# Two decoder layers: one pass over all tokens against two token halves, one behind the other

## The chip, the cores and the metric

The kernel runs on one core of one Trainium2 chip. The metric is the device time of one execution in microseconds (us); lower is better. All times below are of that core. Its engines are named as the profile names them: PE (TensorE, matmuls and transposes; PEld is its weight load), DVE (VectorE), ACT (ScalarE), POOL (GpSimd) and SP (SyncE). Each of them takes its instructions strictly in the order in which the program gives them; a DMA is put into a queue by one of the engines and then runs by itself.

## The reference

Two layers of a decoder run over 1024 prompt tokens and 8 sample tokens (one new token for each of 8 sequences with 1024 cached positions). Cut to what matters:

```python
for l in range(DEPTH):                       # 2 layers, D_MODEL 1024
    n = rmsnorm(yp, norm1[l])
    q, k, v, gq, gk, gv, glog, gg = project(n, w_in[l], ...)   # one input projection, 3088 columns
    od = diff_attn_prompt(q, k, v, lam)      # 4 heads, causal: softmax(q1 k1) - lam softmax(q2 k2), times v
    og, s_fin = gla_prompt(gq, gk, gv, glog) # 4 heads, gated linear attention, a state carried from token to token
    yp = yp + merge(od, og, gg, ...)         # per-head norms, silu gate, ONE output projection w_out
    yp = yp + ffn(yp, norm2[l], w_gu[l], w_down[l])   # SwiGLU, d_ff 2816
    # the 8 sample tokens go through the same weights; their attention reads
    # k and v of 1024 past positions out of a paged cache (page_table), their GLA a given state
```

What matters for the order of the work: the second half of the prompt (tokens 512 to 1023) needs keys, values and the GLA state of the first half. The first half needs nothing of the second. Everything but attention and GLA works on each token by itself.

## The kernel before

Every large product is made exact to nearly float32 by splitting both factors into a high part and the rest (`xH`, `xL` for activations; `wh`, `wl` for weights), and adding three products: high by high, rest by high, high by rest. ACT rounds a weight tile into `wh`, DVE subtracts to get `wl`. So a weight tile costs one DMA (`raw`), one or two ACT and DVE instructions, and then three matmuls for each block of 128 rows and each block of token columns. The "dense" work below means these split products: input projection, output projection and feed-forward network (FFN). "Mix" means attention, GLA and what belongs to the 8 sample tokens (decode): reading cache pages, scores, softmax, weighted values.

A layer (`layer`) runs for all 1032 tokens in four phases.

- `phase_d`: head by head, the q, k, v columns of the input projection (`psq`, 128 tokens by 384 columns, 9 token tiles), QK norm and rotary (`qk`), transposes (`tpqk`), and causal attention of each 128-token tile (`attend`: scores `psS`, softmax in `sc`, transposes `tpw`, values `po`). Attention of a tile is written LAG = 2 tiles behind its projection. Page work of the decode (`decode_k`: `kpg` pages loaded by SP, multiplied by POOL, summed by DVE) is spread between by KRATE.
- `phase_g`: GLA. Products `psqk`, `psv`, `psgg` (the dense part of it), and `gla_a`, `gla_o`, `decode_softmax`, `decode_v`, `sample_gla`, called in an order written out by hand. Matmuls `psA`, `poG`, `puG`, `psov`, `psgn` are its mix.
- `out_phase`: output projection into `psf` (three blocks of 344 token columns, CH = 344), residual added.
- `ffn_phase`: chunks of 3 or 4 blocks of 128 hidden features: gate, up, Silu, down, all into `psf`. Weight tiles come through `prep_tile` (L977): rings of 3 `raw`, 3 `wh` and 2 `wl` tiles.

In `phase_d` and `phase_g` the engines have dense and mix work side by side. In `out_phase` and `ffn_phase` there is dense work alone. The order on each engine follows the order of the code, with a scheduler that lets an instruction that is free go ahead of one that waits; once fixed, it doesn't change at run time. Nearly all DMAs, weights, cache pages and results, go through SP's queue; POOL issues two.

Of the kernel before, what the change touches and what calls it, by code (L numbers as in the profile page):

```python
# [28 lines left out]
CH = TOK // 3  # L29
# [8 lines left out]
NPB = 5  # L38
KPB = 4
LAG = 2  # L40
GRH = 3
KRATE = (0, 2, 1, 3)
# [8 lines left out]
BIG = 3.0e38  # L51

# [6 lines left out]
def hybrid_kernel(  # L59
# [9 lines left out]
    w_queues = (ACT, SP, SP)  # L69

    const = ctx.enter_context(tc.tile_pool(name="const", bufs=1))
    dram = ctx.enter_context(tc.tile_pool(name="dram", bufs=1, space=DRAM))

    def cst(name, shape, dt=F32):
        return const.tile(shape, dt, name=name, tag=name)

# [9 lines left out]
    last_silu = []  # L86
    preload = []

    def load_ln_exp():
        with ExitStack() as st:  # L90
            if last_silu:
                st.enter_context(tc.issue_after(last_silu[-1].ins))
            preload.append(ACT.preload_act_table_set("natural_log_exp_and_others"))

    def after_preload(ins):
        tc.add_manual_dep(ins.ins, preload[-1].ins.name,
                          mybir.DependencyInfo(mybir.DependencyClass.NoSync, mybir.DependencyReason.DATA), reason="act table")

# [6 lines left out]
    def bc(ap, shape):  # L105
        return ap.to_broadcast(shape)

# [12 lines left out]
    xH = cst("xH", [P, KD, TOK], F32R)  # L120
    xL = cst("xL", [P, KD, TOK], F32R)
    xs = cst("xs", [P, KD, 40], F32R)
    POOL.memset(f(xs), 0.0)
    ssq = cst("ssq", [P, TOK])
    rstd = cst("rstd", [P, TOK])
    rcol = cst("rcol", [P, NT + 1])
    r2 = cst("r2", [P, NT + 1])
    lnr = cst("lnr", [P, NT + 1])
    lnm = cst("lnm", [P, NT + 1])

# [3 lines left out]
    load_ln_exp()  # L134
# [14 lines left out]
    ssqc = cst("ssqc", [P, NT + 1])  # L149

    def col_stats(rows, cols, src, scale):
        after_preload(act(lnm[rows, cols], src, AF.Ln, scale=scale, bias=eps_t[rows]))
        act(rcol[rows, cols], lnm[rows, cols], AF.Exp, scale=-0.5)
        act(r2[rows, cols], lnm[rows, cols], AF.Exp, scale=-1.0, bias=nln64[rows])
        act(lnr[rows, cols], lnm[rows, cols], AF.Copy, scale=-0.5)

    def rms_rows(pool, psp, tag, ttag="nrt"):
        for t in range(3):
            sl = slice(t * CH, (t + 1) * CH)
            ps = psp.tile([P, 512], F32, name="nrm", tag=tag)  # L160
            mm(ps[:, :CH], ones_dm, ssq[:, sl], True, True)
            tmp = pool.tile([P, CH], F32, name="nrt", tag=ttag, bufs=1)
            after_preload(act(tmp, ps[:, :CH], AF.Ln, bias=eps_t))
            act(rstd[:, sl], tmp, AF.Exp, scale=-0.5)

    def rms_cols(pool, psp, tag):
        ps = psp.tile([P, 512], F32, name="nrc", tag=tag)
        for i in range(NT):
            mm(ps[:, i:i + 1], ssq[:, i * P:(i + 1) * P], ones_dm[:, 0:1], True, True)
        mm(ps[0:NB, NT:NT + 1], ssq[:, SEQ:TOK], ones_dm[:, 0:1], True, True)  # L170
        for rows, cols in ((slice(0, P), slice(0, NT)), (slice(0, NB), slice(NT, NT + 1))):
            col_stats(rows, cols, ps[rows, cols], 1.0)

    def prep_cols(wps, l, c0, ns, w, step, q=SP, gr=False, width=None):
        Hs, Ls = [], []
        n = ns * w + (RANK if gr else 0)
        width = width or n
        for k in range(KD):
            raw = wps[0].tile([P, width], F32, name="raw", tag="raw", bufs=4)
            if ns == 1:  # L180
                q.dma_start(raw, w_in[l, k * P:(k + 1) * P, c0:c0 + w])
            else:
                b0 = c0 - c0 % step
                q.dma_start(raw[:, :ns * w].rearrange("p (s c) -> p s c", s=ns),
                            w_in[l, k * P:(k + 1) * P, b0:b0 + ns * step]
                            .rearrange("p (s c) -> p s c", s=ns)[:, :, c0 % step:c0 % step + w])
            if gr:
                q.dma_start(raw[:, ns * w:n], w_in[l, k * P:(k + 1) * P, C_GR:C_GR + RANK])
            wh = wps[1].tile([P, width], F32R, name="wh", tag="wh", bufs=9)
            wl = wps[2].tile([P, width], F32R, name="wl", tag="wl", bufs=9)  # L190
            g = g1c[:, l, k:k + 1]
            act(wh[:, :n], raw[:, :n], AF.Copy, scale=g)
            stt(wl[:, :n], raw[:, :n], g, f(wh[:, :n]), ALU.mult, ALU.subtract)
            Hs.append(wh)
            Ls.append(wl)
        return Hs, Ls

    def gemm_tok(ps, n, Hs, Ls, i):
        for k in range(KD):
            if i < NT:  # L200
                ts = slice(i * P, (i + 1) * P)
                mm(ps[:, :n], xH[:, k, ts], Hs[k][:, :n], k == 0, False)
                mm(ps[:, :n], xL[:, k, ts], Hs[k][:, :n], False, False)
                mm(ps[:, :n], xH[:, k, ts], Ls[k][:, :n], False, k == KD - 1)
            else:
                mm(ps[0:40, :n], xs[:, k, :], Hs[k][:, :n], k == 0, False)
                mm(ps[0:40, :n], xs[:, k, :], Ls[k][:, :n], False, k == KD - 1)

    def gemm_feat(ps, c0, Hs, Ls, t):
        ts = slice(t * CH, (t + 1) * CH)  # L210
        for k in range(KD):
            mm(ps[:, :CH], Hs[k][:, c0:c0 + P], xH[:, k, ts], k == 0, False)
            mm(ps[:, :CH], Hs[k][:, c0:c0 + P], xL[:, k, ts], False, False)
            mm(ps[:, :CH], Ls[k][:, c0:c0 + P], xH[:, k, ts], False, k == KD - 1)

    scr_q = [dram.tile([NB, H * 2 * DK], F32, name=f"scr_q{l}") for l in range(DEPTH)]
    scr_sn = [dram.tile([NB, 2 * H], F32, name=f"scr_sn{l}") for l in range(DEPTH)]
    scr_gv = [dram.tile([NB, H * DV], F32, name=f"scr_gv{l}") for l in range(DEPTH)]
    scr_v = [dram.tile([NB, H * DV], F32, name=f"scr_v{l}") for l in range(DEPTH)]
    scr_x = [dram.tile([KD, P, TOK], F32, name=f"scr_x{l}") for l in range(DEPTH)]  # L220
    scr_oh = [dram.tile([H, P, SEQ], F32, name=f"scr_oh{l}") for l in range(DEPTH)]
    scr_ol = [dram.tile([H, P, SEQ], F32, name=f"scr_ol{l}") for l in range(DEPTH)]

    smp = ctx.enter_context(tc.tile_pool(name="smp", bufs=1))

    page_dma = []

    def layer(l):
        sn = smp.tile([NB, 2 * H], F32, name="sn", tag="sn")
        osd = smp.tile([P, H, NB], F32, name="osd", tag="osd")  # L230
        if l:
            sample_cols()

        with ExitStack() as octx:
            with ExitStack() as mix:
                pgp = mix.enter_context(tc.tile_pool(name="pgp", bufs=1, reuse_waits="tile", side="right"))
# [96 lines left out]
    def phase_d(l, dctx, sn, pgp):  # L333
# [241 lines left out]
        for u in todo:  # L575
            decode_k(*u)
# [649 lines left out]
```

## Time and profile before

| what | value |
|---|---|
| median of 3 runs | 2929.18 us (2926.89 to 2933.85) |
| the profiled execution | 2924.06 us; its span, first to last instruction, 2922.3 us |
| mean granted TensorE clock | 0.975 of full speed |
| busy share of the span | PE 94%, PEld 90%, DVE 55%, ACT 39%, POOL 14% |
| DMA | 236.34 MB, 81 GB/s on the mean |

Read the table as an average over unlike stages: each layer has some 603 us of `phase_d` and `phase_g`, where all engines are busy, and some 850 us of `out_phase` and `ffn_phase`, where PE alone is. "Busy" counts a matmul that runs at half clock for as long as it takes, so a busy PE is not PE at its best.

### The profile page before, as it was taken

The page shows a single profiled execution, that of the slowest core. Times are in us where ns is not written, and L with a number is a line of the kernel's source. Part 1 is how long each engine was busy: PE and PEld are TensorE (multiplying, and loading weights), DVE is VectorE, ACT ScalarE, POOL GpSimd, SP SyncE. Part 2 cuts the span into 40 slices and gives each one's busy share as a digit, 9 for nine tenths or more (in the row PEclk, how much of TensorE's full clock was granted, in tenths as well). Part 3 has the DMA queues.
Part 4 walks back from the last instruction along what each step waited for, and adds up shares of the span by engine and source line. Part 5 has one row for each costly group of instructions (what it writes and reads, how often), then busy time and mean ns, then how long its engine had stood idle before and what let it go on. Part 6 is the DMA issues. An engine that isn't in the chain of part 4 may idle for free. (4 is left out here: it accounts for less than half of the span.)

```text
span 2922.3 us, 46249 instructions
## 1 busy us (share of the span) xinstructions
PE 2753.5 (94%) x16910; PEld 2616.2 (90%) x16910; DVE 1615.0 (55%) x3159; ACT 1146.4 (39%) x2960; POOL 404.9 (14%) x340
## 2 busy tenths in 40 slices
PE   8998898889999999999988988988899999999999
PEld 7787788789999999999977777877899999999998
DVE  7898887964333333333478988689543333333332
ACT  7787535652111111112377874356421111111112
POOL 1232423311000000000113233143110000000000
PEclk9999999999999999999999999999999999999999
DMA  4343414453011121212023333235531121211112
GB/s 136 91 132 92 136 37 117 129 177 134 27 55 57 33 62 33 62 30 69 23 85 96 109 112 106 55 112 149 165 123 37 40 62 33 62 37 55 47 40 77
DMA packets 320134, 236.34 MB, mean 81 GB/s; under 512 B 26122, under 2 KB 293642, under 8 KB 319906
## 3 DMA queue, kind: packets, MB, share of 16 engines
q1 hardware_dynamic: 311138, 229.16, 26.5%
q10 hardware_dynamic: 8704, 4.20, 0.6%
q8 instruction: 133, 2.18, 0.3%
q14 instruction: 95, 0.78, 0.1%
q0 software_dynamic: 64, 0.03, 0.0%
HBM read 201.33 MB, written 31.98 MB: 80 GB/s over the span
## 5 line engine op out<-in xcount | busy, mean ns | idle before, releaser
L78 PE MATMUL psf<-xH,wh 128*128 128x344 f32 x2112 | 676.1, 320 | 0.0
L78 PE MATMUL psf<-xH,wl 128*128 128x344 f32 x2112 | 674.7, 320 | 0.0
L78 PE MATMUL psf<-xL,wh 128*128 128x344 f32 x2112 | 674.5, 320 | 0.0
L84 ACT ACTIVATE wh<-raw 128x512 fp32r<-128x512 f32 (+1 forms) x304 | 178.1, 616 | 1113.1 <-PE psf L78 1099.6
L78 PEld LDWEIGHTS psf<-xH,wh 128*128 128x128 f32 x2112 | 396.6, 188 | 0.6 <-ACT xH L84 0.4
L78 PEld LDWEIGHTS psf<-xH,wl 128*128 128x128 f32 x2112 | 396.9, 188 | 0.2
L78 PEld LDWEIGHTS psf<-xL,wh 128*128 128x128 f32 x2112 | 396.6, 188 | 0.4
L78 PE MATMUL psf<-hh,wl 128*128 128x344 f32 x1056 | 338.5, 321 | 0.0
L78 PE MATMUL psf<-hh,wh 128*128 128x344 f32 x1056 | 338.3, 320 | 0.0
L78 PE MATMUL psf<-hl,wh 128*128 128x344 f32 x1056 | 338.2, 320 | 0.0
L100 DVE TENSOR_TENSOR acc<-psf,acc 128x1032 f32<-128x1032 f32 x96 | 118.3, 1233 | 301.6 <-PE psf L78 301.6
L100 DVE TENSOR_TENSOR tb<-psf,rstd 128x1032 f32<-128x1032 f32 x44 | 54.2, 1233 | 389.2 <-PE psf L78 389.2
L100 POOL TENSOR_TENSOR kpg<-kpg,qbd 128x512 f32<-128x512 f32 x128 | 170.6, 1340 | 438.2 <-DMA qbd<-scr_q 147.9
L100 DVE TENSOR_TENSOR wl<-raw,wh 128x512 fp32r<-128x512 f32 (+1 forms) x304 | 204.9, 690 | 13.1 <-PE psf L78 12.1
L100 DVE TENSOR_TENSOR sa<-psf,rstd 128x1032 f32<-128x1032 f32 x44 | 54.2, 1233 | 274.8 <-PE psf L78 274.8
L78 PEld LDWEIGHTS psf<-hh,wh 128*128 128x128 f32 x1056 | 198.6, 188 | 0.2 <-DVE acc L100 0.2
L78 PEld LDWEIGHTS psf<-hh,wl 128*128 128x128 f32 x1056 | 198.4, 188 | 0.3 <-DVE wl L100 0.3
L78 PEld LDWEIGHTS psf<-hl,wh 128*128 128x128 f32 x1056 | 198.3, 188 | 0.0
L78 PE MATMUL psq<-wh,xH 128*128 128x384 f32 (+1 forms) x512 | 183.1, 358 | 5.3 <-ACT v L84 3.9
L78 PE MATMUL psq<-wl,xH 128*128 128x384 f32 (+1 forms) x512 | 183.2, 358 | 2.7 <-DVE wl L103 2.7
L78 PE MATMUL psq<-wh,xL 128*128 128x384 f32 (+1 forms) x512 | 181.7, 355 | 0.0
L78 PE MATMUL psf<-oL,wh 128*128 128x344 f32 x384 | 126.2, 329 | 0.0
(319 smaller groups left out, 5468.4 us busy)
## 6 DMA issues: line engine op xcount, KB each, us to landing
raw<-in_w_gu SPq DMA_DIRECT2D x88, 512.0 KB
kpg<-in_cache_k SPq DMA_DIRECT2D x256, 128.0 KB
page<-in_cache_v SPq DMA_DIRECT2D x128, 256.0 KB
raw<-in_w_down SPq DMA_DIRECT2D x64, 256.0 KB
raw<-in_w_in SPq DMA_DIRECT2D x64, 192.0 KB
scr_x<-og SPq DMA_DIRECT2D x16, 516.0 KB
acc<-scr_x SPq DMA_DIRECT2D x16, 516.0 KB
raw<-in_w_in SPq DMA_DIRECT2D x64, 128.0 KB
```

The lines of the kernel that those rows point to most:

```text
L78: PE.matmul(out, lhsT=lhsT, rhs=rhs, start=start, stop=stop, skip_group_check=True)
L84: return ACT.activation(out, in_, func, **kw)
L100: (eng or DVE).tensor_tensor(out, a, b, op=op)
```

## The change

The tokens are split into two halves, X = 0 (512 tokens) and X = 1 (512 and the 8 sample tokens, 520 columns, taken as two blocks of 260). Each phase is a function of layer and half: `phase_p` (all of the input projection: q, k, v and the GLA columns), `phase_t` (the mix: `attention` and `gla`, decode with X = 1), and `phase_of` (output projection and FFN). The mix of one half is issued beside dense work of the other. Since the halves of two phases now live side by side, nothing is handed over in SBUF any more. `phase_p` writes q, k, v, GLA inputs and gates to DRAM (`scr_qk`, `scr_v`, `scr_g`, `scr_gv`, `scr_gr`, `scr_gg`); `phase_t` reads them back through POOL's queue (`TQ = POOL`) and writes its results split into `scr_oh`, `scr_ol`; `phase_of` reads those on SP's queue (16 loads). The residual stays in DRAM (`scr_x`).

Where an instruction of the mix falls between dense ones is decided by a number, its priority: `dense(us)` and `mix(us)` advance two clocks by the length that the author writes for each piece, and `mix_window(start, rate)` sets where the mix of a half begins on the dense clock and how fast it runs against it.

The weights are loaded and split once for each half, so twice a layer. PSUM is split into two double banks for dense work (`psD`) and four banks for mix (`psM`). Rings are shorter: LAG 2 to 1, `kpg` 4 to 3, `page` 5 to 4, `raw` of `prep_tile` 3 to 2. FFN chunks are 4, 4, 4, 4, 4, 2 blocks, and the Silu of each chunk is followed by a reload of the table of Ln and Exp on ACT (49 table loads in place of 4).

```diff
-NPB = 5
-KPB = 4
-LAG = 2
+NPB = 4
+KPB = 3
+LAG = 1
-KRATE = (0, 2, 1, 3)
...
+HALF = 512
+COLS = (HALF, HALF + NB)
+WM = HALF + NB
+SUBS = (((0, HALF),), ((0, WM // 2), (WM // 2, WM)))
+TILES = ((0, 1, 2, 3), (4, 5, 6, 7, NT))
+TICK = 20
+WINDOWS = ((20.0, 1.0), 0.7, 1.0, 0.7)
...
+    def dense(us):
+        tc.cur_priority = 1000 + int(clock["dense"] * TICK)
+        clock["dense"] += us
+
+    def mix(us):
+        tc.cur_priority = 1000 + int(clock["mix"] * TICK)
+        clock["mix"] += us * clock["rate"]
+
+    def mix_window(start, rate):
+        clock["mix"], clock["rate"] = start, rate
...
+    TQ = POOL
...
+                def start():
+                    for x in range(X + 1):
+                        kt[x] = ap.tile([P, 2, 512], F32R, name="kt", tag="kt", bufs=X + 2)
+                        vt[x] = ap.tile([P, 4, DV], F32, name="vt", tag="vt", bufs=X + 2)
+                        TQ.dma_start(vt[x], scr_v[l][x][h].rearrange("(i p) d -> p i d", p=P))
+                    if X:
+                        TQ.dma_start(f(kt[0]), scr_kt[l][h])
...
+    def phase_t(l, X, start, rate):
+        mix_window(start, rate)
...
+            attention(l, X, sall)
+            gla(l, X, sall)
...
-        raw = wps[0].tile([P, KD, P], F32, name="raw", tag="raw", bufs=nb)
-        SP.dma_start(raw[:, :nk, :], src)
+        raw = wps[0].tile([P, KD, P], F32, name="raw", tag="raw", bufs=2)
+        SP.dma_start(raw[:, :nk, :], src.rearrange("(k p) c -> p k c", p=P))
...
+                for k in (3, 0, 1, 2, 4, 5, 6, 7):
+                    SP.dma_start(f(oH[:, k, :W]), scr_oh[l][X][k])
+                    SP.dma_start(f(oL[:, k, :W]), scr_ol[l][X][k])
...
+                    si = act(sa[:, :n, :W], sa[:, :n, :W], AF.Silu)
+                    load_ln_exp(si)
...
+        phase_p(0, 0, s, xH, xL)
+        phase_t(0, 0, *WINDOWS[0])
+        phase_p(0, 1, s2, xH2, xL2)
+    t = clock["dense"]
+    phase_t(0, 1, t, WINDOWS[1])
+    s = phase_of(0, 0)
+    phase_p(1, 0, s, xH, xL)
+    t = clock["dense"]
+    phase_t(1, 0, t, WINDOWS[2])
+    s = phase_of(0, 1)
+    phase_p(1, 1, s, xH, xL)
+    t = clock["dense"]
+    phase_t(1, 1, t, WINDOWS[3])
+    phase_of(1, 0)
+    phase_of(1, 1)
```

So T(0,0) is issued beside P(0,1), T(0,1) beside OF(0,0) and P(1,0), T(1,0) beside OF(0,1) and P(1,1), T(1,1) beside OF(1,0), and OF(1,1) by itself (P, T and OF for the three phases, with layer and half).

On PE, before, this is the place where layer 0 goes from GLA to its output projection: the gate products `psgg`, the last decode values (`psov`) and norms (`psgn`, `pson`), and `psf` is the output projection.

```order
2291 L78 MATMUL psgg<-xL,wh 128x344
2292 L78 MATMUL psov<-ones_66,vacc 128x1 x8
2293 L78 MATMUL psgn<-gsq,ones_dv 128x16
2294 L78 MATMUL psf<-oH_9006,wh 128x344
2295 L78 MATMUL psgn<-gsq,ones_dv 128x512
2296 L78 MATMUL psf<-oL_9008,wh 128x344
2297 L78 MATMUL psf<-oH_9006,wl 128x344
2298 L78 MATMUL psf<-oH_9006,wh 128x344
```

After the change, PE at the start of OF(0,0): `psd` is any dense product, here the output projection of half 0, and `tpqk`, `psS` are transposes and scores of attention of half 1.

```order
2020 L96 MATMUL psd<-xH_170,wl 128x260
2021 L96 MATMUL psd<-oH,wh 128x512
2022 L96 MATMUL psd<-oL,wh 128x512
2023 L96 MATMUL psd<-oH,wl 128x512
2024 L96 MATMUL psd<-oH,wh 128x512
2025 L99 MATMUL tpqk<-ident,qk 128x128 x2
2026 L96 MATMUL psd<-oL,wh 128x512
2027 L96 MATMUL psd<-oH,wl 128x512
2028 L96 MATMUL psd<-oH,wh 128x512
2029 L99 MATMUL tpqk<-ident,qk 128x128 x2
2030 L96 MATMUL psd<-oH,wh 128x512
2031 L96 MATMUL psS<-kt,qhh 128x512
```

Mix steps that stood beside input projections now stand one by one between dense products of the output projection and the FFN, and dense products behind such a step come after it on PE.

On POOL, before, this is the end of the decode values of layer 0 and the start of its FFN (`ssq` are sums of squares for the next norm, `wa` a gate weight).

```order
79 L100 TENSOR_TENSOR vacc<-vacc,vaccp 128x512
80 L100 TENSOR_TENSOR vaccp<-vaccp,page 128x512 x3
81 L100 TENSOR_TENSOR vacc<-vacc,vaccp 128x512
82 L100 TENSOR_TENSOR ssq<-ssq,og 128x1032 x7
83 L100 TENSOR_TENSOR ssq<-ssq,acc 128x1032 x4
84 L532 DMA wa_15744<-in_w_a 16x256
```

After, POOL in T(0,1): `qk`, `vt`, `kt` are the handover read back from DRAM, `qbd` the query of a sample token, `kpg` the multiplication of cache pages.

```order
95 L537 DMA vt<-scr_v_126 128x4x128
96 L544 DMA qk<-scr_qk_123 128x256 x2
97 L539 DMA kt<-scr_kt_120 128x1024
98 L105 TENSOR_TENSOR kpg<-kpg,qbd 128x512 x4
99 L509 DMA qbd<-scr_q_112 128x256
100 L105 TENSOR_TENSOR kpg<-kpg,qbd 128x512
101 L544 DMA qk<-scr_qk_123 128x256
102 L105 TENSOR_TENSOR ssq<-ssq,nsq 128x512
103 L105 TENSOR_TENSOR kpg<-kpg,qbd 128x512 x3
```

DMA issues that POOL did not have before stand behind its multiplications; POOL has 486 rows in place of 162, about 290 of them DMA issues.

On SP, after, within the FFN of OF(0,0): `raw` is a weight tile of the down product, `page` a value page of the cache. Before, no page load stands between two weight loads of the FFN.

```order
2153 L493 TENSOR_LOAD pt_sb
2154 L493 ISA x2
2155 L494 ISA
2156 L494 DMA page<-in_cache_v 128x512
2157 L1007 DMA raw<-in_w_down 128x4x128
2158 L493 TENSOR_LOAD pt_sb
2159 L493 ISA x2
2160 L494 ISA
2161 L494 DMA page<-in_cache_v 128x512
```

Weight loads now wait in SP's queue behind page loads; at 19 places 4 to 9 of them, and at one place, before the first weight of OF(0,1), 50, stand between two weight loads.

## Rows read from the trace of the kernel before

**Rows 1.** The page's first part: the span, and each engine's busy time and share.

```profile
span 2922.3 us, 46249 instructions
...
PE 2753.5 (94%) x16910; PEld 2616.2 (90%) x16910; DVE 1615.0 (55%) x3159; ACT 1146.4 (39%) x2960; POOL 404.9 (14%) x340
```

**Rows 2.** Windows by stage: length, busy us (instructions) of each engine, clock, DMA share, GB/s.

```profile
0.00:603.00 603.00, 529.67 (x3105) 465.27 (x3105) 506.57 (x1256) 398.94 (x1242) 174.25 (x160) 0.95 0.39 111
...
1461.00:2064.00 603.00, 523.28 (x3050) 459.36 (x3051) 505.18 (x1235) 391.48 (x1214) 179.75 (x158) 0.94 0.38 110
...
2166.00:2916.00 750.00, 749.02 (x4764) 746.23 (x4764) 244.03 (x275) 134.34 (x194) 0.00 (x0) 1.00 0.18 54
```

**Rows 3.** PE's timeline: start, duration, line, operation, tile, shape.

```profile
202.90 0.34 PE L78 MATMUL psq<-wl,xH 128*128 128x384 f32 x1
...
205.70 0.34 PE L78 MATMUL psq<-wh,xH 128*128 128x384 f32 x1
...
220.82 0.39 PE L78 MATMUL psS<-kt,qhh 128*128 128x512 f32 x1
221.05 0.40 PE L78 MATMUL psS<-kt,qlz 128*128 128x512 f32 x1
...
369.49 0.28 PE L78 MATMUL psv<-wh,xL 128*128 128x256 f32 x1
...
370.78 0.28 PE L78 MATMUL psv<-wh,xH 128*128 128x256 f32 x1
...
372.35 1.13 PE L78 MATMUL psA<-xqz,gD 128*128 128x128 f32 x8
373.24 0.36 PE L78 MATMUL psv<-wl,xH 128*128 128x256 f32 x1
```

**Rows 4.** The chain that ended last, in order of time: start, us, what.

```profile
2064.62 90.01 PE psf L78 x570
...
2166.67 706.18 PE psf L78 x4483
...
2911.47 3.79 PE psf L78 x24
```

**Rows 5.** PE's waits in 1461:2064: who waited for whom; total us, times, longest.

```profile
PE tpqk L81 <- DVE qk L100: 14.6, 12, 4.6
PE tpw L81 <- DVE sc L103: 9.1, 14, 2.5
```

**Rows 6.** Windows of two short stretches, columns as in group 2.

```profile
146.00:219.00 73.00, 68.93 (x379) 59.32 (x378) 69.55 (x201) 62.05 (x216) 27.37 (x20) 1.00 0.47 131
600.00:610.00 10.00, 4.02 (x25) 3.97 (x23) 8.63 (x17) 5.75 (x17) 4.62 (x4) 0.66 1.00 341
```

**Rows 7.** Groups by line and shape: count, busy us, mean ns, idle before.

```profile
L100 DVE TENSOR_TENSOR wl<-raw,wh 128x512 fp32r<-128x512 f32 x272 | 187.4, 707 | 13.1 <-PE psf L78 12.1 <-issue 0.8
L84 ACT ACTIVATE wh<-raw 128x512 fp32r<-128x512 f32 x272 | 161.3, 626 | 953.1 <-PE psf L78 939.7 <-issue 7.6 <-DMA raw<-in_w_gu 3.5
L100 DVE TENSOR_TENSOR acc<-psf,acc 128x1032 f32<-128x1032 f32 x96 | 118.3, 1233 | 301.6 <-PE psf L78 301.6
L93 ACT ACT_TABLE_LOAD x2 | 2.6, 1283 | 0.8 <-PEq L1210 0.7
```

**Rows 8.** One line's operations: duration in ns, least, median, longest; first, last start.

```profile
L262 SPq DMA_DIRECT2D page<-in_cache_v x128: 332/333/742, 422.9 to 2044.7; - x128
...
L261 SPq TENSOR_LOAD <-pt_sb x384: 261/268/872, 35.3 to 2043.9; - x192
L261 SPq FUSED_REGOPS  x384: 147/152/181, 35.9 to 2044.2; - x192
```

**Rows 9.** POOL's own DMAs and its page multiplication, columns as in group 8.

```profile
L532 POOL DMA_DIRECT2D wa<-in_w_a x2: 546/609/672, 3.3 to 1451.2; - x2
...
DMA to landing us min/median/max: 2.0/3.0/4.0
...
L100 POOL TENSOR_TENSOR kpg<-kpg,qbd x128: 1261/1288/2254, 110.6 to 1788.2; 128x512 f32<-128x512 f32 x128
```

More of the change, by code (lines that the diff above doesn't have):

```diff
@@ L106, in bc, with load_ln_exp, after_table @@
         return ap.to_broadcast(shape)
+    clock = {"dense": 0.0, "mix": 0.0, "rate": 1.0}
+    def dense(us):
[6 more added lines that the diff above has]
+        clock["mix"], clock["rate"] = start, rate
+    def load_ln_exp(after=None):
+        with ExitStack() as st:
+            if after is not None:
+                st.enter_context(tc.issue_after(after.ins))
+            return ACT.preload_act_table_set("natural_log_exp_and_others")
+    first_table = load_ln_exp()
+    def after_table(ins):
+        tc.add_manual_dep(ins.ins, first_table.ins.name,
+                          mybir.DependencyInfo(mybir.DependencyClass.NoSync, mybir.DependencyReason.DATA), reason="act table")
     ident = cst("ident", [P, P])
@@ L148, in hybrid_kernel @@
     subg1 = cst("subg1", [P, DEPTH])
[L149 to L226, printed above, removed]
@@ new lines, in attention, with pop @@
+            pending = []
+            def pop():
+                us, fn = pending.pop(0)
+                mix(us)
+                fn()
+                decode_some(4)
+            for h in (3, 0, 1, 2):
+                start, prep, attend, finish = head(h)
+                mix(1)
+                start()
+                for i in range(4):
+                    mix(2.5)
+                    prep(i)
+                    pending.append((2 + 1.6 * (TILES[X][i] + 1), lambda a=attend, i=i: a(i)))
+                    while len(pending) > LAG:
+                        pop()
+                pending.append((4, finish))
@@ new lines, in hybrid_kernel @@
+    s = Stats()
+    with ExitStack() as bs:
+        xb = left(bs, "xb")
+        xH2 = xb.tile([P, KD, WM], F32R, name="xH2", tag="xH2")
+        xL2 = xb.tile([P, KD, WM], F32R, name="xL2", tag="xL2")
+        dense(1)
+        load_x(0, xb, s, xH, xL)
+        rms_load(s, 0)
+        with ExitStack() as ls:
+            load_consts(ls)
+        s2 = Stats()
+        clock["dense"] = 70
+        dense(0)
+        load_x(1, xb, s2, xH2, xL2)
+        rms_load(s2, 1)
+        sample_cols(xH2, xL2)
+        clock["dense"] = 10
+        phase_p(0, 0, s, xH, xL)
+        phase_t(0, 0, *WINDOWS[0])
+        phase_p(0, 1, s2, xH2, xL2)
```

1598 lines of the change are left out of this document (812 added, 786 removed).

## The prediction

> **What bounds the kernel now.** I read the page's first part first: PE is busy 94% of the span, DVE 55%, ACT 39% [rows 1]. At face value little is left to win. But busy is not work: a matmul at half clock counts double. So next come the windows by stage [rows 2]. From 2166 on PE is busy 749.02 of 750 us at clock 1.00 with 4764 matmuls, that is .157 us each, and nothing else is half as busy: here PE's own speed is the bound and nothing can be gained without taking matmuls away. In attention and GLA (0 to 603, and 1461 to 2064 for layer 1) PE is busy 523 to 530 of 603 us, and at clock .94 to .95. The chain of waits says the same: in the last stage two pieces of PE alone carry nearly all of it [rows 4]. So all that can be won lies in the two stretches of 603 us.
>
> How much? PE's timeline gives the step of each kind of matmul when they follow each other without a gap [rows 3]: sixteen steps of 384 columns from 202.90 to 205.70 are .175 us each, 512 columns (220.82 to 221.05) .23, eleven steps of 256 columns .117, eight of the small GLA ones .111. A layer has 832 matmuls of 384 columns (146 us), 416 of 256 columns (49), 576 of 344 columns (90), and mix (attention, GLA, decode, transposes) that comes to about 170 by counting at .1 to .23 each, an estimate. That is 455 us of work in a stretch of 603: **148 us lost in each layer, 296 in both**. The rest of the run, 2924 - 2 x 603 = 1718, is 1673 of `psf` work (10,656 matmuls at .157), some 20 of transposes and norms, 8 at the start of the first output projection (600:610 has PE at 4.02 of 10), some 3 at the norms, and 9 at the end (last matmul over at 2915.26, span 2922.3, run 2924.06) [rows 1, 4, 6]. So work is about 2 x 455 + 1693 = 2,600, and the account closes to within 10 us.
>
> Why is it lost there? PE's waits there are short and many, and nearly all on DVE or ACT: `tpqk` on `qk`, `tpw` on the softmax [rows 5]. PE, in order, waits in the middle of attention's chain of small steps, and with a granted clock of .94 on the mean, between its levels of 1.2 and 2.4 GHz, it runs a part of the stretch at the lower one [rows 2]. Where enough dense work stands between, it needn't be so: from 146 to 219, attention beside projections, PE is busy 68.93 of 73 us at clock 1.00, though DVE is busy 69.55 [rows 6]. So 5.6% lost is possible beside attention, against 148 of 603, 25%, as things are.
>
> **The change part by part.**
>
> *Matmuls.* The same products over the same columns. A weight tile's three products over a third of the tokens cost 3 x .157 = .47 us for 344 + 344 + 344 columns; in halves they are one of .23 (512) and two of 260, which by the 256-column step are .12 each: .47. No change. Work stays at 2,600.
>
> *Weights twice.* Each weight tile is split a second time. FFN and output projection: 272 pieces of DVE at 707 ns and of ACT at 626 ns [rows 7]; with the smaller forms I add 303 us to DVE and 261 to ACT. Forty-five more table loads at 1283 ns are 58 on ACT [rows 7]. DVE comes to about 1,920 us, ACT to 1,465, of some 2,840: both below PE. DVE is hidden behind PE as long as no stretch has it near full. Adding the order's rows at these durations, the opening stretch has DVE 297 beside PE 320, T(0,1) 440 beside 515, T(1,1) 600 beside 800: no stretch where DVE is the longer. DMA grows from 236 to about 400 MB (102 of weights, 60 of handover), 140 GB/s on the mean, where a window shows 341 [rows 6].
>
> *Where the loss goes.* Mix beside dense now spans PE work of 320 + 515 + 493 + 800 = 2,128 us, with OF(1,1), 473, alone after it. The gap per mix step can be filled by dense products of the FFN, which need nothing of it. Best case by rows 6: 5.6 of 94.4, so 126 us over the contested stretch. Worst that is no mechanism of its own: the 296 stay. I take **148**, half of today's, close to the fed slice but not at it, because LAG is 1 in place of 2 and rings are shorter.
>
> *Starts of OF.* Four in place of two, each with 16 loads of 256 KB, 4.2 MB; at 341 GB/s [rows 6] that is 12.3 us. In layer 0 before, the same start cost 8. Now a mix may run meanwhile, in three of four. Bounds 0 and 12.3; I take 10 each, **40**.
>
> *Norm joints.* Four pairs in place of two, each half as long; before, the gate products of the first chunk cover them. **10** for all.
>
> *Page loads ahead of weights.* On SP one page costs .333 + .268 + .152 = .75 us [rows 8], so eight between two weight loads, as the order shows, are 6.0 us. The PE work of a gate unit is 24 x .23 = 5.5, of a down unit 12 x .23 = 2.8, and two `raw` tiles stand ahead. Gate units hide it; down units lose some .5 to 1 at each of 19 places: **16**. A page load that has to wait for a free buffer makes it more; that is in the slower rival.
>
> *Start and end.* Before, the first wait for tokens is in the 296; **13** more for P(0,0), whose weights are first split with no mix beside them, and **9** at the end as before.
>
> *Handover.* Results are stored well before they are read (on PE, T(0,1) ends at row 3933, the first product of OF(0,1) that uses it stands at 4851), so the way through DRAM itself costs nothing. What POOL pays: its two DMA issues took .61 us of the engine, landing 3.0 later [rows 9]; 290 are 177 us more on POOL, beside 405 busy [rows 1]. That is hidden behind a span of 2,840 unless a read is late: 3.0 us for each of 4 tiles of a head is covered by rings of 3.
>
> Rows 9 also hold the one hint against it: `kpg` takes 1,288 ns on the median, 2,254 at most, 1 us more, about one long DVE instruction (the split of 512 columns is .707, the eviction of 1,032 is 1.233) [rows 7]. The Trainium skill, page SBUF — State Buffer, sections "SBUF: two separate sides" and "Who interferes with whom", says that POOL itself makes the descriptors of the DMAs that it issues, and that it is locked out while some forms of DVE's instructions run. The spread of `kpg` agrees with such a lock; no run here shows it for a DMA. By the rule these 290 would be the wrong queue.
>
> **Sum.** 2,600 + 148 + 40 + 10 + 16 + 13 + 9 = 2,836; I say **2,840**. The profiled run before took 2924, so 3% less; the median shown is 2929.18, 5 us above that run, within what runs differ. What a measurement can tell from no change is about 0.2%, 6 us.
>
> **The rivals.**
>
> *A. Better overlap.* The fed slice repeated, and OF starts hidden by mix: loss of 74 (a quarter), starts 0: 2,836 - 74 - 40 = 2,722. For it: FFN products are 2,000 us of cover for 340 of mix. Against it: the slice is 73 us picked as the best one, and 126 is what it gives when scaled. I put 2,700 to 2,790 here. Chance .12.
>
> *B. Slower: PE's queue waits inside the mix.* The order is fixed by lengths that the author wrote in; PE has one queue. A mix step whose softmax is 3 us late now stops dense work behind it, FFN too, which before ran at 749 of 750. DVE also has FFN evictions of up to 1.23 us [rows 7] and twice the splits in its queue between the steps of a softmax, so each step of attention's chain comes later than before. If the 296 stay, the sum is 2,836 + 148 = 2,984; it decides against the change once the loss is over 148 + 88 = 236, 80% of today's (the sum then is 2924). Page loads that wait in front of weights add to it. For it: DVE at 85% beside T(0,1). Against it: the fed slice had DVE at 95% and lost 5.6%. Chance .23.
>
> *C. Slower: POOL's queue.* In-order POOL puts a read of `qk` behind multiplications of 1.3 us that themselves wait for pages, and behind sums `ssq`. If each of the 290 costs attention .61 us on the path it is 177, if each waits for one eviction of 1.233 us [rows 7], 357: 3,010 to 3,190. For it: `kpg`'s spread [rows 9]. Against it: reads are issued a tile ahead, and much of T is slack beside dense work. Chance .12.
>
> *D. No change*, gain and added costs in balance: within 0.2% of 2924, .06.
>
> **How the numbers follow.** Forecast .47 (its own range 2,790 to 2,915), A .12, D .06, B .23, C .12. Faster by over 0.2%: .47 + .12 = .59; same .06; slower .35. The range must leave out no more than 2 in 10: low 2,730 leaves out the better part of A, high 3,010 takes in B with the whole loss kept and leaves out C, some .06 and .13.
>
> **What would show it.** Right: windows over T with clock .98 or more and PE over 93% busy, PE busy time falling by some 100 us from 2753.5 because fewer matmuls run at half clock; OF(1,1) as dense as 2166:2916; DVE near 1,920, ACT near 1,465. B right: PE's waits in T(0,1) and T(1,1) on `sc`, `qk` or `xqz` adding to over 150 us. C right: waits of PE or ACT on loads of `qk`, `vt`, `kt` or `qbd`, and POOL DMA landings far over 3.0 us. Wrong in another way: waits on `wl` or `raw` in the FFN over 40 us in all, which would mean that the weight path, not the mix, sets the time; or PE at clock 1.00 and yet long, which would mean that I missed work.

## The result and the profile after

The changed kernel takes 3173.65 us (median of 4 runs, 3163.03 to 3184.68), the kernel before 2928.03 beside it: **8.4% slower**, ratio 1.084 (1.079 to 1.089). The forecast was 2,840 and 3% faster. The profiled execution has a span of 3161.3 us.

The page's first part of the changed kernel, against [rows 1]:

```profile
span 3161.3 us, 49911 instructions
...
PE 2828.1 (89%) x16904; PEld 2480.1 (78%) x16904; DVE 1862.5 (59%) x3759; ACT 1479.7 (47%) x3505; POOL 602.6 (19%) x656
...
DMA packets 570145, 427.45 MB, mean 135 GB/s; under 512 B 50506, under 2 KB 514218, under 8 KB 569890
```

PE has 16,904 matmuls in place of 16,910, so no matrix work was added. DVE, ACT and DMA came out near the sums made for them (1,920, 1,465, 400 MB). Of 239 us more span, PE's busy time took 75 and its idle time 164; the mean granted clock fell from .975 to .940, so that as many matmuls kept PE busy for longer. By the prediction's own count of work, 2,600, the run loses 561 us, where the sum had 236.

Windows of the changed kernel: three stretches of T(0,1) beside OF(0,0), then most of OF(1,1) (columns as in group 2 of the rows).

```profile
500.00:715.00 215.00, 180.93 (x769) 140.83 (x769) 168.96 (x321) 95.11 (x172) 113.60 (x100) 0.93 0.59 175
720.00:860.00 140.00, 137.87 (x628) 109.42 (x628) 81.26 (x163) 74.59 (x129) 2.96 (x5) 1.00 0.25 74
860.00:1100.00 240.00, 209.96 (x952) 166.01 (x951) 173.74 (x346) 113.21 (x265) 103.70 (x109) 0.88 0.54 161
...
2800.00:3100.00 300.00, 300.00 (x2506) 300.00 (x2505) 134.15 (x209) 94.20 (x136) 0.00 (x0) 1.00 0.31 89
```

This is the place to read twice. OF(1,1) alone is as dense as hoped. From 720 to 860 attention of half 1 runs beside the FFN, and PE is busy 98% at clock 1.00: the idea of the change works there. From 500 to 715 it is the same attention, first beside the output projection and a norm joint and from about 565 beside the same FFN, and PE falls to 84% and .93; from 565 on alone it is 129.41 of 150 us, 86%, at .94. What the first stretch has and the second hasn't is the decode's page work: POOL is busy 113.60 us in it, against 2.96. From 860 on it is GLA with the value pages, POOL at 103.70, and PE falls as far, to 87% and .88.

PE's waits in the changed kernel (columns as in group 5):

```profile
PE psd L96 <- POOL ssq L105: 40.4, 6, 17.7
PE psd L99 <- DMA xt<-in_x_prompt: 36.3, 7, 15.9
PE psS L96 <- DVE mx L583: 33.8, 15, 7.0
PE psd L96 <- DMA oH<-scr_oh: 26.8, 5, 15.2
PE psov L96 <- POOL vacc L105: 25.2, 10, 5.4
PE tpw L99 <- DVE sc L108: 20.9, 24, 3.7
PE psd L96 <- DVE wl L105: 18.4, 16, 5.5
```

The largest sum is new (2.9 us in all before): in six places, in front of each FFN and of each input projection of layer 1, PE stands at the norm product, waiting for POOL's sums of squares. POOL's and PE's timelines around the longest of the six:

```profile
2115.90 1.26 POOL L105 TENSOR_TENSOR kpg<-kpg,qbd 128x512 f32<-128x512 f32 x1 [4.58 <-DMA kpg<-in_cache_k]
2117.43 1.42 POOL L105 TENSOR_TENSOR ssq<-ssq,nsq 128x512 f32<-128x512 f32 x1 [0.27 <-ACT nsq L102]
2118.82 1.71 POOL L105 TENSOR_TENSOR kpg<-kpg,qbd 128x512 f32<-128x512 f32 x1
2120.49 1.25 POOL L105 TENSOR_TENSOR ssq<-ssq,nsq 128x512 f32<-128x512 f32 x1
...
2121.80 2.07 PE L96 MATMUL psd<-ssq,ones_dm 128*128 128x512 f32 x2 [17.67 <-POOL ssq L105]
```

POOL, in order, stands 4.58 us at a multiplication whose page hasn't landed, with the sums behind it. The other five waits are 3.8 to 6.1 us each.

And what DVE's instructions take, in the changed kernel from 500 to 715, then from 720 to 860 (groups by line and shape: busy us, mean ns):

```profile
L105 DVE TENSOR_TENSOR wl<-raw,wh 128x512 fp32r<-128x512 f32 x48 | 49.1, 1044 | 3.1 <-PE psd L96 3.0
L105 DVE TENSOR_TENSOR acc<-psd,acc 128x1024 f32<-128x1024 f32 x8 | 9.7, 1218 | 4.7 <-PE psd L96 4.7
L105 DVE TENSOR_TENSOR hl<-tb,hh 128x1024 fp32r<-128x1024 f32 x2 | 3.6, 1811 | 0.0
...
L105 DVE TENSOR_TENSOR wl<-raw,wh 128x512 fp32r<-128x512 f32 x37 | 24.8, 687 | 10.4 <-issue 5.9 <-PE psd L96 4.4
L105 DVE TENSOR_TENSOR acc<-psd,acc 128x1024 f32<-128x1024 f32 x5 | 6.1, 1222 | 6.9 <-PE psd L96 6.9
L105 DVE TENSOR_TENSOR hl<-tb,hh 128x1024 fp32r<-128x1024 f32 x4 | 4.9, 1221 | 0.5 <-ACT hh L102 0.5
```

The split of a weight tile takes 1,044 ns on the mean in the stretch where POOL multiplies pages and 687 in the other; `hl`, which also reads two tiles of SBUF, 1,811 and 1,221. `acc`, which takes one of its inputs from PSUM, stays at 1,218 and 1,222. So it is not that DVE is slow there, but that one kind of its instructions is held up. Counted one by one in the whole trace, the 497 splits of this shape that overlap no two-input instruction of POOL take 684 ns on the mean, and the 79 that overlap one take 1,175, the longest 2,891. In the GLA stretch, 860 to 1100, the split takes 774, so there the hindrance is smaller, though PE loses as much.

### The profile page after: what moved, and what is told of

Its sections match the earlier page's. It is cut to its first block, busy times and chain, and to the rows that moved or that the text cites. A ratio compares the mean times of both kernels' runs of the same rounds, so it can differ in the third digit from the quotient of the medians.

```text
span 3161.3 us, 49911 instructions
## 1 busy us (share of the span) xinstructions
PE 2828.1 (89%) x16904; PEld 2480.1 (78%) x16904; DVE 1862.5 (59%) x3759; ACT 1479.7 (47%) x3505; POOL 602.6 (19%) x656
## 4 chain that ended last, share of the span: by engine, by line
PE 57%; DVE 13%; DMA 11%; issue 6%; ACT 6%; POOL 4%; SPq 2%; POOLq 0%; DVEq 0%; ACTq 0%
PE psd L96 48%; DVE wl L105 2%; DMA kpg<-in_cache_k 2%; DMA raw<-in_w_in 2%; PE po L96 2%; PE psA L96 1%; POOL kpg L105 1%; ACT wh L102 1%; DMA raw<-in_w_gu 1%; DVE acc L105 1%; PE psS L96 1%; DMA page<-in_cache_v 1%; DVE tb L105 1%; DVE vacc L108 1%; PE tpw L99 1%
## 5 line engine op out<-in xcount | busy, mean ns | idle before, releaser
L96 PE MATMUL psd<-xH,wh 128*128 128x260 f32 (+1 forms) x2496 | 825.3, 331 | 11.3 <-ACT wh L102 11.1
L96 PE MATMUL psd<-xH,wl 128*128 128x260 f32 (+1 forms) x2496 | 819.4, 329 | 7.0 <-DVE wl L108 4.3
L96 PE MATMUL psd<-xL,wh 128*128 128x260 f32 (+1 forms) x2496 | 815.9, 327 | 0.0
L96 PEld LDWEIGHTS psd<-xH,wh 128*128 128x128 f32 x2496 | 481.7, 193 | 53.6 <-ACT wh L102 13.5
L96 PEld LDWEIGHTS psd<-xH,wl 128*128 128x128 f32 x2496 | 480.2, 193 | 46.8 <-DVE wl L108 6.1
L96 PEld LDWEIGHTS psd<-xL,wh 128*128 128x128 f32 x2496 | 479.9, 192 | 38.8 <-issue 3.5
L96 PE MATMUL psd<-hh,wh 128*128 128x260 f32 (+1 forms) x1056 | 355.4, 337 | 13.7 <-ACT hh L102 10.7
L96 PE MATMUL psd<-hh,wl 128*128 128x260 f32 (+1 forms) x1056 | 350.0, 332 | 15.9 <-DVE wl L105 15.8
L96 PE MATMUL psd<-hl,wh 128*128 128x260 f32 (+1 forms) x1056 | 348.5, 330 | 0.9 <-DVE hl L105 0.7
L96 PE MATMUL psd<-wh,xH 128*128 128x384 f32 (+2 forms) x768 | 258.3, 336 | 7.5 <-ACT v L102 3.1
```

Source lines behind the costliest of these rows:

```text
L96: PE.matmul(out, lhsT=lhsT, rhs=rhs, start=start, stop=stop, skip_group_check=True)
```

## The experiments

Theories, named as in the expectations: **M**, DVE's amount of work and PE's fixed order (rival B of the prediction). **C**, POOL's queue is late (its rival C). **P**, weights wait on SP behind page loads. **J**, the norm joints. **O**, the opening. **S**, what is lost depends on how close the mix steps stand; its rival is **F**, a fixed price for each step. **L**, the shorter lag. **K**, formed after the first twelve runs: POOL's work on SBUF lengthens DVE's instructions. Times are medians, with the ratio to the kernel before, which ran beside each; the changed kernel's is 1.084 (1.079 to 1.089). That interval is 15 us to either side, so a gain of less than about that much over 3,174 can't be told from none.

**1. Joints.** The norm product moves from ahead of the first gate products to behind the first group of them.

```diff
-                    tt(s.ssq[:, :W], s.ssq[:, :W], sq[:, :W], ALU.add, POOL)
+                    tt(s.ssq[:, :W], s.ssq[:, :W], sq[:, :W], ALU.add)
-                rms_rows(s2, X)
...
+                        if c == 0 and fs[0] == 0:
+                            rms_rows(s2, X)
```

> Edit: the sum of squares is added on DVE in place of POOL, and the norm product that opens each FFN stands behind the first gate products. The changed kernel's time is 3,174 us; its PE waits 40.4 us in 6 places for POOL's sums. Theory J (these joints cost what their waits show, and some more because PE falls to the lower clock after them): 3,110 to 3,135. Rival M (the time is set by the chain of small attention steps anyway, and what is saved at a joint is lost at the next step): within 15 us of 3,174.

3,136.5, ratio 1.071 (1.066 to 1.075): 37 us less, just outside the range named, and as much as the waits themselves. The wait for `ssq` falls from 40.4 to 5.1. J holds; the further gain by the clock did not show. The edit moves two things, the sums to DVE and the norm product behind the gate products; which of them gave the gain is not separated.

**2. Second splits.** `prep_tile` skips the subtraction when X is 0.

```diff
+            if split:
                 tt(wl[:, ks, :], raw[:, ks, :], f(wh[:, ks, :]), ALU.subtract)
```

> Leaves out part of the computation: in output projection and FFN of half 0, the rest of the weights is not computed, and the product that takes it uses the high part again; matmuls stay as many, DVE has about 150 us less, all of it beside attention, GLA and decode of half 1. Theory M (DVE, with twice the splits in its queue, is late for the mix steps that PE waits for): 80 us or more less than 3,174, waits of PE for mx, sc and xqz at most half. Rival P (page loads hold up the weights): under 30 us less.

3,095.1, ratio 1.056 (1.053 to 1.059): 79 us less, at the bound named. DVE's busy time falls by 191 us (1862.5 to 1671.8), not 150. But the waits that M named did not halve: those for `mx` went from 33.8 to 22.7, those for `xqz` from 14.4 to 15.9, those for `sc` rose from 20.9 to 37.2. M's time came, the fall of the waits by which it was to come did not.

**3. No page loads, with a new constant.** A constant tile of 2 KB a partition takes the place of the pages.

> Leaves out part of the computation: no cache page is loaded, the decode's products and sums stay and read one constant tile. SP's queue then has weights and results alone. Rival P (weights wait behind page loads, and the mix behind pages): 100 us or more less than 3,174, and ACT's waits for weight tiles, 315.6 us for gate and up, at most half. Theory M (DVE and PE's order set the time): under 40 us less.

3,549.8, ratio 1.212 (1.209 to 1.215), against both theories. The reason is in the order on PE: with this tile all mix of T(0,1), and of T(1,1), stands at one place with no dense product between. So the run priced something else, the mix of half 1 by itself. A window in the middle of it:

```profile
600.00:700.00 100.00, 54.10 (x178) 37.74 (x179) 72.83 (x196) 46.85 (x97) 57.66 (x59) 0.66 0.16 46
```

PE is busy half of the time, and at clock .66. Set beside the 3,159.6 of run 6, which also loads no page but reads a constant that is there already, having the mix of half 1 stand between dense products is worth 390 us here. That the 2 KB left no room for both halves' buffers is likely and was not looked at further.

**4. No decode page work at all.**

> Leaves out part of the computation: all page work of the decode, loads as well as products and sums on POOL, ACT and DVE. What it gives beyond the run without page loads is the price of the decode's arithmetic in the mix. Theory M: the decode's 300 us of DVE work is what makes DVE late, so 100 us or more beyond the run without page loads. Rival P: most of the gain is there without the loads already, under 40 us beyond it. If neither run gains 60 us, the loss lies in attention and GLA themselves.

3,015.0, ratio 1.030 (1.028 to 1.033): 159 us less, and 145 below run 6, which M named (100 or more). So most of the excess goes with the decode's page work. But this kernel leaves out work that the kernel before does, and is still 87 us slower than it: the halves lose time without the decode too.

**5. The opening.** The second half's tokens are loaded after the first head's projections.

> Edit: the tokens of the second half are loaded and transposed after the first head's projections of the first half, not before them; all else stays. In the changed kernel PE waits 36.3 us for tokens in the first 60 us, and granted clock is .74 in the first 100. Theory O (the opening is lost outright, the prediction's 13 us for it was too small): 3,130 to 3,145. Rival (the first projections wait for their split weights anyway): within 15 us of 3,174.

3,162.8, ratio 1.081 (1.078 to 1.084): 11 us less, within what the runs can tell from none, and within the rival's bounds. PE's waits for tokens fell from 36.3 to 19.2 us, so the edit priced 17 us of them and not all; the rest of the opening is not priced by it.

**6. No page loads, memory unchanged.** As run 3, with a constant that the kernel has anyway; the mix stands where it does in the changed kernel.

> Leaves out part of the computation: no cache page is loaded, the decode's products and sums stay and read a constant that is there already, so that no memory is added; the run before this one had 2 KB more in each partition, and its PE order held all of T(0,1) and of T(1,1) in one piece with no dense product between. Here the mix steps stand where they do in the changed kernel. Rival P (weights and mix wait for pages on SP's queue): 80 us or more less than 3,174. Theory M (DVE's load and the order on PE): under 40 us less.

3,159.6, ratio 1.080 (1.078 to 1.083): 14 us less. P falls. Together with run 4: not the loads cost, but what is done with the pages.

**7. Wider spacing.**

```diff
-WINDOWS = ((20.0, 1.0), 0.7, 1.0, 0.7)
+WINDOWS = ((20.0, 1.0), 1.0, 2.0, 0.7)
```

> Edit: the rates of T(0,1) and T(1,0) are 1.0 and 2.0 in place of 0.7 and 1.0, so that the same mix steps stand among 537 and 480 us of dense work on PE in place of 376 and 250. T(1,1), which has no more room, stays. Theory S (what is lost depends on how close the mix steps stand): 3,085 to 3,130. Rival F (each mix step costs its wait wherever it stands): within 20 us of 3,174. The prediction took the mix as spread over 2,128 us of dense work.

3,165.1, ratio 1.082 (1.079 to 1.084): 9 us less. S falls, F holds: the same steps among half as much dense work again, or twice as much, lose the same.

**8. Handover on SP's queue.**

```diff
-    TQ = POOL
+    TQ = SP
```

> Edit: the handover is read and written through SP's queue in place of POOL's (one word); POOL then has arithmetic alone. Rival C (POOL's queue is late, for its sums, its page products and its DMAs): 60 us or more less than 3,174, and waits of PE for ssq, vacc and vb at most half of 80 us. Theory M: POOL's lateness is a small part, and a load that waits on SP for a free buffer now holds up the weights behind it: 3,150 to 3,300.

3,147.7, ratio 1.075 (1.071 to 1.079): 26 us less, so both missed: M's range began at 3,150. PE's wait for `ssq` is 24.4 in place of 40.4, for `vacc` 19.7 in place of 25.2. POOL's queue was late for its sums, as C says, at well under half of C's price.

**9. Edits 1, 5 and 8 together.**

> Edits: the three correct single edits that gained together: sums on DVE with the norm product behind the first gate products (38 us alone), tokens of the second half later (11), handover on SP's queue (26). Theory A (three separate losses): 3,174 - 75 = 3,085 to 3,115. Rival (they recover the same waits): 3,125 to 3,140. In no case under 2,928: the mix stages keep most of their loss.

3,120.7, ratio 1.066 (1.064 to 1.068): 53 us less in place of 75, between the two. Edits 1 and 8 recover in part the same joint.

**10. The same without the second splits of half 0.**

> Leaves out part of the computation: as the run with the three edits together, and the rest of half 0's weights in output projection and FFN is not computed (DVE 190 us less, beside the mix of half 1). Theory M, DVE's load beside the mix costs PE time by itself: 60 us or more less than the three edits together. Rival: what DVE's load cost was waits at the joints and for POOL, which are gone already: under 30 us less.

3,055.8, ratio 1.043 (1.041 to 1.045): 65 us below run 9. The second splits cost by themselves, not through the joints.

**11. Value pages from DVE to ACT and POOL.**

```diff
-VPOOL = (0, 2, 4, 6)
+VPOOL = (0, 2, 3, 4, 6, 7)
```

> Edit: six of eight value pages of a sample token go to ACT and POOL in place of four, so DVE has some 50 us less of decode work, ACT and POOL as much more. Theory M (DVE): 15 to 35 us less than 3,174. Rival C (POOL is what is late, PE waits 25 us for its sums): 10 us or more slower.

3,168.3, ratio 1.082 (1.080 to 1.084): no change; neither theory's range was met. DVE has 128 instructions fewer and yet its busy time did not fall (1862.5 to 1864.5): in the GLA stretch, 860 to 1100, the split of a weight tile rose from 774 to 937 ns. What was taken off DVE came back in the time of its other instructions.

**12. LAG 2.**

> Edit: LAG is 2 again: attention of a tile is written two tiles behind its transposes, with a ring more of each. Theory L (the shorter lag leaves too little between a step and the step that needs it): 20 us or more less than 3,174, waits of PE for mx and sc at most two thirds of 55 us. Rival M (DVE is late as a whole, a step more between doesn't help): within 15 us.

3,159.9, ratio 1.079 (1.076 to 1.082): 14 us less, within the rival's bounds. The shorter lag is not the cause.

So runs 2 and 10 speak for M, and run 11, which was meant to test it, did not lower DVE's busy time. The windows and DVE lines shown above gave theory K, which the next runs test.

**13. No products of key pages on POOL.** One column of 256 is left.

> Leaves out part of the computation: of POOL's 128 multiplications of key pages only one column in 256 stays, so that the order of load, product and sum is kept; DVE's sums stay. Theory K (while POOL works on SBUF, DVE's instructions with two SBUF inputs take longer): the split of a weight tile in the stretch from 500 us on falls from 1,044 ns to under 720, and the kernel gains 30 us or more. Rival M (it is DVE's own amount of work): within 15 us of 3,174, since DVE has as many instructions as before.

3,120.5, ratio 1.067 (1.064 to 1.070): 53 us less, with every DVE instruction still there. The split from 500 to 715 in this run:

```profile
L105 DVE TENSOR_TENSOR wl<-raw,wh 128x512 fp32r<-128x512 f32 x56 | 39.4, 725 | 7.4 <-PE psd L96 4.4 <-issue 2.6 <-ACT wh L102 0.3
```

From 1,044 to 725 ns, just over the bound of 720 that was named. K's gain came, M's forecast of none did not.

**14. The same products on DVE**, all of them.

```diff
-                tt(pg, pg, bc(qbs[hp].unsqueeze(1), [P, 2, 256]), ALU.mult, POOL)
+                tt(pg, pg, bc(qbs[hp].unsqueeze(1), [P, 2, 256]), ALU.mult)
```

> Edit: the key pages are multiplied on DVE in place of POOL, 128 instructions more on DVE of .7 us each, 90 us in all. Theory K: DVE gets this back from its other instructions, and the kernel is 0 to 40 us faster. Rival M: 35 us or more slower (second splits cost .4 us for each us of DVE).

3,123.0, ratio 1.068 (1.065 to 1.071): 51 us less, a little more than K's range, though DVE does 128 products more. The stretch from 500 to 715 in this run, by lines:

```profile
L105 DVE TENSOR_TENSOR kpg<-kpg,qbd 128x512 f32<-128x512 f32 x57 | 39.5, 699 | 14.3 <-DMA kpg<-in_cache_k 14.0
L105 DVE TENSOR_TENSOR wl<-raw,wh 128x512 fp32r<-128x512 f32 x56 | 37.9, 703 | 3.2 <-PE psd L96 3.1
```

and as a window:

```profile
500.00:715.00 215.00, 201.33 (x881) 158.49 (x880) 191.64 (x402) 109.27 (x198) 28.79 (x40) 0.96 0.60 178
```

DVE is busy 191.64 us of 215, more than before the edit (168.96), and PE 201.33 in place of 180.93, with 881 matmuls done in place of 769. DVE's busy share was the wrong thing to look at.

**15. Hardly any sums of key pages on DVE.**

> Leaves out part of the computation: DVE's 256 sums over key pages take 8 of 256 columns, so each falls from .41 to some .1 us, and DVE has about 80 us less beside attention of half 1; POOL's products stay. Rival M: 30 us or more less than 3,174. Theory K: under 20 us, since the sums have one input only and aren't what POOL holds up.

3,164.1, ratio 1.081 (1.078 to 1.084): no change to speak of, with some 65 us less on DVE (256 sums of 152 in place of 408 ns). The split still takes 971 ns. As K says.

**16. Value pages on PE, on run 9.**

> Edit, on the kernel with the three correct edits (3,121): value pages are multiplied by their weights on PE, 32 products of one column for each sample token, in place of ACT, POOL and DVE; PE has some 50 us of work more, DVE 107 less, POOL some 100 less. Theory K and M both: PE's waits for vacc go, and the stretch of GLA loses less: 3,080 to 3,120 in all, PE's own 50 us set against it. Rival (PE then waits for the pages themselves): over 3,135.

3,236.6, ratio 1.107 (1.104 to 1.110), 116 us above run 9. PE's waits for `vacc` are gone, but PE's busy time rose by 148 us (2827.9 to 2975.5), not 50:

```profile
L96 PE MATMUL psov<-wall,page 128*128 128x1 f32 x1024 | 158.4, 278 | 0.0
```

512 products appear as 1,024 matmuls, each with a weight load of its own for one column. The estimate had 512. The rival's time came for another reason than the one named.

**17. The three edits and the key products on DVE.**

> Edits: the three correct edits together (3,121) and the key pages' products on DVE (51 us alone). Theory A (adds to them): 3,065 to 3,085. Rival (the same waits are recovered): 3,100 to 3,121. Over 2,928 in any case: the stages of half 1 still lose what their chain of steps costs.

3,076.6, ratio 1.052 (1.050 to 1.055): 44 us below run 9, so it adds. This is the cleaner price of the products on POOL, since runs 13 and 14 shorten something else as well: PE's wait for `ssq`, 24.4 and 22.5 in place of 40.4, nearly all at the one place of 17.67 shown above (1.2 and 1.3 there). In run 9 these sums are off POOL already.

A rival of K that no expectation names is DVE's own place in order: it waits for POOL's products in front of its page sums (`sall` for `kpg`, 99.3 us in all in the changed kernel, 89.8 in run 9), with splits and softmax behind. Run 6 answers it: without page loads that wait falls to 32.8 us, the split still takes 905 ns from 500 to 715, and the kernel gains 14 us. DVE's wait in the changed kernel, then in run 6, and the split in run 6 from 500 to 715:

```profile
DVE sall L515 <- POOL kpg L105: 99.3, 54, 5.7
...
DVE sall L515 <- POOL kpg L105: 32.8, 45, 1.9
...
L105 DVE TENSOR_TENSOR wl<-raw,wh 128x512 fp32r<-128x512 f32 x48 | 42.6, 905 | 9.8 <-PE psd L96 5.3 <-issue 4.0 <-ACT wh L102 0.4
```

**18. POOL's sums of value pages on DVE too**, on run 17.

```diff
-                            tt(accp, accp, p4, ALU.add, POOL)
+                            tt(accp, accp, p4, ALU.add)
-                tt(acc, acc, accp, ALU.add, POOL)
+                tt(acc, acc, accp, ALU.add)
```

> Edit, on e17: POOL's sums over value pages go to DVE as well, 48 instructions in each layer, some 35 us more of DVE in all. Theory K (POOL's work on SBUF costs DVE more than the work itself): 10 us or more less than e17. Rival (it holds for key pages alone, since there the FFN's weight splits meet it): within 10 us of e17 or slower.

3,052.6, ratio 1.043 (1.042 to 1.045): 24 us below run 17, as K says; the split in the GLA stretch falls from 765 to 691 ns. Not all of the 24 need be K's: PE's waits for POOL's `vacc`, 11.6 us in run 17, are gone too. It is the fastest of the forms that compute everything, and still 4.3% slower than the kernel before. The window of the same stretch in this run:

```profile
500.00:715.00 215.00, 204.52 (x917) 159.74 (x916) 194.06 (x410) 113.00 (x206) 0.00 (x0) 1.00 0.60 179
```

and its page's first part:

```profile
PE 2792.5 (91%) x16904; PEld 2448.5 (80%) x16904; DVE 1905.0 (62%) x3993; ACT 1482.2 (49%) x3505; POOL 92.7 (3%) x122
```

The stretch that had PE at 84% and clock .93 has it at 95% and 1.00, and POOL has next to nothing left to do.

The sizes fit. Add up, over all of DVE's instructions that overlap one of POOL's, what they take beyond the median of their shape without overlap: an estimate from the traces, some 98 us in the changed kernel and 57 in run 14, 88 in run 9, 48 in run 17 and 11 in run 18. The falls of 40, 40 and 37 stand beside gains of 51 (some 16 of them at the norm joint), 44 and 24.

## Why the prediction was wrong

**The step that failed** is "Weights twice": "DVE is hidden behind PE as long as no stretch has it near full". From 500 to 715 DVE was busy 79%, and PE paid for it all the same. The second splits of half 0, at nothing in the sum, cost 65 to 79 us (runs 10 and 2). The page products, moved from POOL to the busier DVE, gave 44 us back (run 17; 51 in run 14, with a norm joint in it), and POOL's sums at most 24 more (run 18). The step took DVE's durations as fixed. They are not: on the mean of a stretch in which POOL computes nearly half of the time, an instruction with two inputs from SBUF takes half as long again. Whether the second splits cost time as DVE's work or as the very instructions that POOL holds up, runs 2 and 10 can't tell.

The Trainium skill, page SBUF — State Buffer, section "Who interferes with whom", states just this: a DVE instruction with two SBUF inputs contends with a GpSimd instruction that reads SBUF, and one with at most one SBUF input, outside the 2-port modes, does not. This case's trace agrees, 1,044 against 687 ns and `acc` unchanged. The prediction cited that section, and took from it what POOL and its DMAs lose, not what DVE loses.

The hindrance itself is not new. By the estimate used under run 18, POOL held up DVE for some 130 us in the kernel before, more than the 98 in the changed one. What the change moved is where it falls: the weight splits of output projection and FFN (304 pieces before, 608 now) met none of POOL's page work before, and eight of them its sums `ssq`; their share of the time lost is some 39 us in place of 6. The products were not moved to DVE in the kernel before, so no run shows how much of the difference between the two kernels, rather than of the changed kernel's own time, is owed to K.

It could have been read beforehand. This is the line of the weight split of the input projection in the trace of the kernel before (least, median, longest ns), which was not among the rows:

```profile
L103 DVE SCALAR_TENSOR_TENSOR wl<-raw,g1c,wh x160: 447/512/2401, 11.4 to 2029.4; 128x256 fp32r<-128x256 f32 x96, 128x384 fp32r<-128x384 f32 x48, 128x400 fp32r<-128x400 f32 x16
```

A longest of 2,401 beside a median of 512, in the stages where POOL works. The line mixes three shapes; of the 48 pieces of 384 columns alone, the 38 that overlap no two-input instruction of POOL take 596 to 622 ns, the other ten 606 to 2,401. The spread of `kpg` [rows 9] fits this from the other side, which no run tested by itself.

**Where the loss goes**, 148, is the term that came out too small, with B's "the 296 stay" as its worst case. The run lost 561 in all; less joints (40), the first OF products' waits (28) and the page bursts and the end (23), some 470 remain for the mix and the opening. B had the sign and the fixed order right, and run 7 shows its core: a step costs the same however far apart the steps stand. The 2,128 us over which the sum spread the mix was also wrong; in the order on PE it stands in some 1,290 us of dense work, an estimate, but by run 7 this cost nothing. B's mechanism, waits for `sc`, `qk`, `xqz` of over 150 us, was not there: with `mx` they come to some 70.

**Norm joints**: 10 in the sum, 37 by run 1. They were taken as half as long each and covered. What was missed is that PE comes to six such places and waits for POOL's sums at each; at one of them, 17.67 of the 40.4 us, they stand in POOL's queue behind products that wait for pages.

**Handover**: nothing in the sum, 26 by run 8, in part the same waits (run 9). Rival C's time, 3,010 to 3,190, holds the result, but its mechanism doesn't: the reads landed 2.8 to 6.3 us after issue for `vt`, and PE waited 1.1 us in all for `qk`.

**Right in size**: page loads ahead of weights, 16 in the sum, 14 in run 6, which can hardly be told from none; starts of OF, 40 in the sum, 28 of PE's waits for `oH` and `oL`; OF(1,1) alone, full at clock 1.00; attention beside the FFN without page work, 2% idle at 720 to 860, where the sum allowed 5.6%.

**The start**, 13 in the sum, was too small: in the first 100 us PE gets through 263 matmuls at clock .74, where the kernel before has 475 at .98. Run 5 brings this to 320 at .92 and gains only 11 us, so how much of it the whole run pays is not shown.

**Still open**: nearly half. The result is 334 us above the forecast. Run 18 takes off 121, and by run 10 the second splits some 65 more, an estimate, since a run with both was not made; some 148 remain, and the kernel would still be above 2,928. Run 4, 87 us over the kernel before without any page work, says the same. The GLA stretches keep PE at 205.19 of 240 us at clock .93 (860 to 1100 in run 18), and what holds them there was not separated.

## What to carry to other kernels

Before work of one stage is moved beside another, list what each engine reads and writes there, not only how long it is busy: durations of DVE's two-input instructions taken from a stage where POOL rests don't hold beside one where it works on SBUF. Look at longest against median for the same shape; here a ratio of nearly 4 (2,401 against some 612 ns) was a hindrance that the mean hid. Work that the next stage's norm waits for does not belong in a queue behind work that waits for DMAs, and splitting tokens in halves doubles whatever is done once for each weight.

## What the runs showed of the hardware

POOL's products on SBUF lengthen DVE's instructions with two inputs from SBUF (the weight split: 684 ns on the mean without overlap, 1,175 with it) and not those with one input from PSUM (`acc`: 1,218 and 1,222 ns) nor the sums with one input (`sall`: 408 ns beside them). The same product takes 1,409 ns on the mean on POOL (500 to 715, changed kernel) and 699 on DVE (run 14), and moving 128 of them to the busier engine made the kernel 51 us faster. In run 16 a product of one column in float32 appears as two matmuls with a weight load each, .15 us of PE's busy time for each of them.
